# The adaLN rows at the start of a decoder trunk: full-width condition columns, x loaded ahead of w_ada, and another order for the first group

## The chip, the cores and the metric

The kernel runs on one core of a Trainium2 chip. The metric is device time in microseconds from the start to the end of one execution; lower is better.

## What is computed

One layer of a decoder trunk with adaLN conditioning, on 1024 tokens of width 1024, in float32. The change lies at its beginning:

```python
cond = jax.nn.silu(c)                                   # (1, 1024)
mod = cond @ w_ada[layer] + b_ada[layer]                # (1, 6 * 1024)
shift1, scale1, gate1, shift2, scale2, gate2 = jnp.split(mod[:, None, :], 6, axis=-1)
h = rms_norm(x, w_norm1[layer]) * (1.0 + scale1) + shift1
x = x + gate1 * hybrid_mixer(h, w_in[layer], ...)       # h @ w_in, four mixers, @ w_out
h = rms_norm(x, w_norm2[layer]) * (1.0 + scale2) + shift2
x = x + gate2 * hierarchical_moe(h, ...)                # 4 groups of 8 experts, top 2
return rms_norm(x, w_norm_final)
```

Only shift1 and scale1 are needed for the first h, and only they are made in the stage that is changed: 2048 of the 6144 columns of w_ada, 8.4 MB.

## The kernel before

The first stage makes h in transposed form, channels on partitions, as two float32r parts: hH, its rounded value, and hL, the rest. In the same stage the values and gates (272 columns of w_in) are multiplied for all 8 token tiles. Its instructions stand in the order in which the code is written (`tc.manual_schedule()`). Work of later stages that needs nothing of it (the first pieces of w_in, loaded at L134 and split by `split`, L53 and L61) is placed among it by the scheduler.

**x.** `x_load` (L194) brings a tile of 128 tokens; there are 7 buffers, and the two pieces of w_in for the values use the same ones. `x_rows` takes the squares (ScalarE), the root, and scales the rows (VectorE, L246). `x_columns` transposes the tile on TensorE (L253, eight transposes) and copies half of it on ScalarE, half on VectorE (L258) into hT.

**The rows of w_ada.** The 1024 channels go in four groups of 256 (`GS`), group g with 256 columns of shift and 256 of scale. `ada_load(g, q)` brings half of a group's rows of w_ada (L201, two DMAs; three buffers). The product of cond with a group's 512 columns is shared between two engines: for the first `KD = 6` blocks of 128 rows VectorE sums weight times cond into `acc` (`ada_sums`, L210 and L212), and for the last two TensorE multiplies with cond as a stationary operand of one column (`ada_products`). `ada_row` adds the sums over the partitions with a product of `acc` and a column of ones, and ScalarE copies the resulting row out of PSUM (`arow`). `ada_columns` turns the row into columns with four transposes (L232), and VectorE makes shift and scale of them (`sc`, L233 and L235).

**A group's use.** Two ScalarE instructions make hH from hT with scale and shift, two more make the unrounded value, and VectorE subtracts (hL). TensorE then multiplies: `tok_hi`, two products of 128 x 272 for each of 7 token tiles and each of the group's two channel blocks (28 in all), in the middle of which the next group's `ada_products` stand; then that group's `ada_row`; then `tok_lo`, 14 products with hL of the group before. The products with hL are called the low part here, those with hH the wide products, and a float32 product is two records in the trace.

All loads of the stage are issued by SyncE (SP) in one order, which is that of the code.

Of the kernel before, what the change touches and what calls it, by code (L numbers as in the profile page):

```python
# [9 lines left out]
F32 = mybir.dt.float32  # L10
# [9 lines left out]
P = 128  # L20
S = 1024
D = 1024
NT = S // P
KT = D // P
# [12 lines left out]
def hybrid_block_kernel(ctx, tc, x, c, w_in, w_out, w_mix_norm, attn_f_bias, sg_w, sg_b,  # L37
# [4 lines left out]
    nc = tc.nc  # L42
# [9 lines left out]
    def act(o, i, f, **kw):  # L52
        return nc.scalar.activation(o, i, f, **kw)  # L53

    def mm(o, l, r, start, stop):
        return nc.tensor.matmul(o, l, r, start=start, stop=stop)  # L56

    def split(hi, lo, src, eng=None):

        act(hi, src, AF.Copy)  # L60
        (eng or nc.vector).tensor_sub(lo, src, hi.bitcast(F32))  # L61
# [10 lines left out]
    ones = consts.tile([P, P], F32, name="ones")  # L72
# [24 lines left out]
    cond = consts.tile([P, KT], F32, name="cond")  # L97
# [4 lines left out]
    def ps1():  # L102
        return ps.tile([P, 512], F32, name="ps1")

    def pq1():
        return pq.tile([P, 512], F32, name="pq1")
# [45 lines left out]
    def tok_hi(o, w, t, k):  # L152
        wh, wl, n = w
        ts = slice(t * P, (t + 1) * P)
        mm(o[:, :n], hH[:, k, ts], wh[:, k, :n], k == 0, False)
        mm(o[:, :n], hH[:, k, ts], wl[:, k, :n], False, False)

    def tok_lo(o, w, t, k):
        mm(o[:, :w[2]], hL[k // 4][:, k % 4, t * P:(t + 1) * P], w[0][:, k, :w[2]], False, k == KT - 1)
# [21 lines left out]
    with tc.tile_pool(name="st", bufs=1, side="left") as st, tc.tile_pool(name="stx", bufs=7, side="left") as stx, \  # L181
# [7 lines left out]
        xts, was, accs, ada, wraw = {}, {}, {}, {}, {}  # L189
        KD = 6  # L190

        def x_load(t):
            xts[t] = stx.tile([P, D], F32, name="xt", tag="xt")
            nc.sync.dma_start(xts[t], x[t * P:(t + 1) * P])  # L194

        def ada_load(g, q):

            k0, k1 = GS[g]
            was[g, q] = stw.tile([P, 4, 2, (k1 - k0) * P], F32, name=f"wt{k1 - k0}", tag="wt")
            for i in range(2):  # L200
                nc.sync.dma_start(was[g, q][:, :, i], w_ada[q * 4 * P:(q + 1) * 4 * P, i * D + k0 * P:i * D + k1 * P]  # L201
                                  .rearrange("(k p) f -> p k f", p=P))

        def ada_sums(g, k):

            if k == 0:
                accs[g] = st.tile([P, 2, (GS[g][1] - GS[g][0]) * P], F32, name="acc", bufs=2)
            acc, wt = accs[g], was[g, k // 4][:, k % 4]
            if k == 0:
                nc.vector.tensor_scalar(acc, wt, cond[:, k:k + 1], None, op0=OP.mult)  # L210
            else:
                nc.vector.scalar_tensor_tensor(acc, wt, cond[:, k:k + 1], acc, op0=OP.mult, op1=OP.add)  # L212

        def ada_products(g):

            ada[g] = pq1()
            for k in range(KD, KT):
                mm(ada[g][0:1], cond[:, k:k + 1], was[g, k // 4][:, k % 4].rearrange("p i f -> p (i f)"), k == KD, False)

        def ada_row(g):  # L220

            mm(ada[g][0:1], ones[:, 0:1], accs[g].rearrange("p i f -> p (i f)"), False, True)
            ada[g, "row"] = st.tile([1, 512], F32, name="arow", bufs=1)
            act(ada[g, "row"], ada[g][0:1], AF.Copy)

        def ada_columns(g):

            k0, k1 = GS[g]
            ks, n = slice(k0, k1), 2 * (k1 - k0)
            o, row = ada[g], ada[g, "row"]  # L230
            for i in range(n):
                nc.tensor.transpose(o[:, i:i + 1], row[:, i * P:(i + 1) * P], ident[0:1, 0:1])  # L232
            nc.vector.tensor_add(sc[:, :, ks], o[:, :n].rearrange("p (i k) -> p i k", i=2),  # L233
                                 cols[:, 54:70].rearrange("p (i k) -> p i k", i=2)[:, :, ks])
            nc.vector.scalar_tensor_tensor(sc[:, 1, ks], sc[:, 1, ks], 1.0, cols[:, 8 + k0:8 + k1],  # L235
                                           op0=OP.add, op1=OP.mult)

        def values_split(i):
            split(wva[0][:, i * 4:i * 4 + 4], wva[1][:, i * 4:i * 4 + 4], wraw[i])

        def x_rows(t):
            sq = st.tile([P, D], B06, name="sq", bufs=1)
            act(sq, xts[t], AF.Square, accum_out=ss[:, t:t + 1])
            act(rstd[:, t:t + 1], ss[:, t:t + 1], AF.Sqrt, scale=1.0 / D, bias=EPS)
            nc.vector.reciprocal(rstd[:, t:t + 1], rstd[:, t:t + 1])
            nc.vector.tensor_scalar(xts[t], xts[t], rstd[:, t:t + 1], None, op0=OP.mult)  # L246

        def x_columns(t):
            xt = xts.pop(t)
            for hf in range(2):  # L250
                tp = pq1()
                for j in range(4):
                    nc.tensor.transpose(tp[:, j * P:(j + 1) * P],  # L253
                                        xt[:, (hf * 4 + j) * P:(hf * 4 + j + 1) * P], ident)
                dst = hT[hf][:, :, t * P:(t + 1) * P]
                src = tp.rearrange("p (a b) -> p a b", b=P)
                if hf:
                    nc.vector.tensor_copy(dst, src)  # L258
                else:
                    act(dst, src, AF.Copy)  # L260

        def values_load(i):
            wraw[i] = stx.tile([P, 4, 272], F32, name="wraw1", tag="xt")
            o = 0
            for c0, n in ((AV, 260), (MDT, 4), (LI, 8)):
                nc.sync.dma_start(wraw[i][:, :, o:o + n], w_in[i * 512:(i + 1) * 512, c0:c0 + n]
                                  .rearrange("(k p) g -> p k g", p=P))
                o += n

        for t in range(5):  # L270
            x_load(t)
        ada_load(0, 0)
        for t in range(5, 7):
            x_load(t)
        ada_load(0, 1)
        x_load(7)
        values_load(0)
        ada_load(1, 0)
        ada_load(1, 1)
# [14 lines left out]
        nc.vector.tensor_scalar(cond, cond, 1.0, None, op0=OP.add)  # L294
        nc.vector.reciprocal(cond, cond)
        nc.vector.tensor_mul(cond, cond, psc[:, 0:KT])
        for t in range(NT + 1):
            if t < NT:
                x_rows(t)
            if t:  # L300
                x_columns(t - 1)
            if t == 3:
                psc = pq1()
                nc.tensor.transpose(psc[:, :66], rows, ident[:66, :66])
                nc.vector.tensor_copy(cols[:, 8:74], psc[:, :66])
            if t == 7:
                ada_products(0)
            for k in {5: (0, 1), 6: (2,), 7: (3, 4), 8: (5,)}.get(t, ()):
                ada_sums(0, k)
        ada_row(0)  # L310
        values_split(0)
        os = [ps1() for _ in range(PSB)] + [pq1() for _ in range(7 - PSB)]
        NGK = len(GS)
        for g, (k0, k1) in enumerate(GS):
            ks, n = slice(k0, k1), k1 - k0
            if g + 2 < NGK:
                ada_load(g + 2, 0)
                ada_load(g + 2, 1)
            ada_columns(g)
            if g + 1 < NGK:  # L320
                for k in range(KD):
                    ada_sums(g + 1, k)
            if k0 == 4:
                hL.append(hpool.tile([P, KT // 2, S], F32R, name="hL1", tag="hL1"))
            ts, ls = [[z[k // 4][:, k % 4] for k in range(k0, k1)] for z in (hT, hL)]
            for k, a in zip(range(k0, k1), ts):
                act(hH[:, k, :], a, AF.Identity, scale=sc[:, 1, k:k + 1], bias=sc[:, 0, k:k + 1])
            for k, a, l in zip(range(k0, k1), ts, ls):
                act(a, a, AF.Identity, scale=sc[:, 1, k:k + 1], bias=sc[:, 0, k:k + 1])
                nc.vector.tensor_sub(l, a, hH[:, k, :].bitcast(F32))  # L330
            if g == 1:
                values_split(1)

            for k in range(k0, k1):
                for t in range(NT - 1):
                    tok_hi(os[t], wva, t, k)
                if k == k0 and g + 1 < NGK:
                    ada_products(g + 1)
            if g + 1 < NGK:
                ada_row(g + 1)  # L340

            for k in range(*GS[g - 1]) if g else ():
                for t in range(NT - 1):
                    tok_lo(os[t], wva, t, k)
# [828 lines left out]
    with ExitStack() as m4:  # L1173
# [263 lines left out]
        with tc.manual_schedule():  # L1437
# [15 lines left out]
            for t in range(NT):  # L1453
# [6 lines left out]
                if last:  # L1460
                    x1T, f = turned(t - 1)
# [12 lines left out]
                if not last:  # L1474
# [3 lines left out]
                    f = [half(i) for i in range(2)]  # L1478
# [46 lines left out]
                if last:  # L1525
# [6 lines left out]
                    f = half(1)  # L1532
# [12 lines left out]
            t = NT - 1  # L1545
# [10 lines left out]
            a, g, p = r6[0], r6[1], r6[3]  # L1556
# [697 lines left out]
```

## Time and profile before

| | |
|---|---|
| three runs | 1276.84, 1277.37 and 1282.47 us, median 1277.37 |
| the profiled execution | 1279.83 us |
| its span, first to last instruction | 1277.7 us |
| PE busy | 1167.9 us, 91% of the span |
| VectorE (DVE), ScalarE (ACT), GpSimd (POOL) busy | 787.1, 591.2, 302.1 us |
| DMA | 305.48 MB, mean 239 GB/s |
| granted TensorE clock, mean | 0.962 |

The profile is of one execution. All times of rows are microseconds from the start of the span. PE is TensorE's products and PEld its weight loads, which run beside them; products are pipelined and their ends are modelled, so that two neighbours can overlap. A row of the timeline stands for one or several instructions of a kind: start, duration, engine, source line, operation, output and inputs, their shapes, the count, and in brackets the idle time of the engine ahead of it with what ended it. The granted clock is a share of 2.4 GHz.

### The profile page before, as it was taken

What the parts mean: (1) busy time and instruction counts of PE and PEld (TensorE: products, weight loads), DVE (VectorE), ACT (ScalarE), POOL (GpSimd) and SP (SyncE); (2) the same over time, 40 slices, a digit from 0 to 9 for tenths busy, and PEclk for the clock granted to TensorE, in tenths of its full rate; (3) what the DMA queues carried; (4) which work ended last, traced back from release to release, by engine and by line L of the source; (5) the groups of instructions that cost most, each with busy time, mean ns of one, the idle gap of its engine ahead of it and who ended that gap; (6) DMA issues with size and microseconds to landing.
All of it is one profiled execution on the core that took longest, in us unless ns stands there. A gap on an engine that the chain in (4) does not pass through costs nothing. (4 is left out here: it accounts for less than half of the span.)

```text
span 1277.7 us, 18620 instructions
## 1 busy us (share of the span) xinstructions
PE 1167.9 (91%) x6479; PEld 867.1 (68%) x6479; DVE 787.1 (62%) x1457; ACT 591.2 (46%) x913; POOL 302.1 (24%) x305
## 2 busy tenths in 40 slices
PE   5699889999999899999959999899999999999991
PEld 3477677889998788887747744366676657665660
DVE  5656766857743488488878941335654564555674
ACT  5542124354743588344437741224553443554563
POOL 1000000002102277333321942102322132222111
PEclk8899999999999999999969999999999999999996
DMA  9604883232221113575477999999999998999974
GB/s 278 202 17 140 263 276 112 80 86 51 70 64 34 43 62 112 204 267 197 170 295 286 332 325 343 383 390 381 380 386 387 350 385 322 342 368 376 341 267 199
DMA packets 96452, 305.48 MB, mean 239 GB/s; under 512 B 15106, under 2 KB 53756, under 8 KB 71772
## 3 DMA queue, kind: packets, MB, share of 16 engines
q1 hardware_dynamic: 84642, 284.43, 60.4%
q0 software_dynamic: 8464, 17.13, 5.7%
q10 hardware_dynamic: 3242, 2.60, 0.6%
q8 instruction: 57, 0.93, 0.3%
q14 instruction: 47, 0.39, 0.1%
HBM read 283.86 MB, written 32.06 MB: 247 GB/s over the span
## 5 line engine op out<-in xcount | busy, mean ns | idle before, releaser
L56 PE MATMUL ps<-wu,xTs 128*64 128x512 f32 x256 | 121.0, 605 | 1.9 <-DMA wu<-in_w_expert_up_dram 1.9
L56 PE MATMUL ps<-wg,xTs 128*64 128x512 f32 x256 | 120.3, 602 | 2.1 <-DMA wg<-in_w_expert_gate_dram 2.1
L1685 POOL DMA_INDIRECT x_d<-yt,tabi x34 | 62.6, 1841 | 238.7 <-DVE yt L1659 187.6
L56 PE MATMUL ps<-wh,hH 128*128 128x256 f32 (+1 forms) x336 | 97.1, 290 | 12.9 <-ACT hH L53 9.9
L56 PE MATMUL ps<-wl,hH 128*128 128x256 f32 (+1 forms) x336 | 95.6, 285 | 0.0
L56 PE MATMUL ps<-wh,hL 128*128 128x256 f32 (+1 forms) x336 | 93.8, 283 | 0.0
L56 PE MATMUL ps<-hH,wh 128*128 128x512 f32 x224 | 89.0, 397 | 0.4 <-ACT xbc L53 0.4
L56 PE MATMUL ps<-hH,wl 128*128 128x512 f32 x224 | 89.1, 398 | 0.0
L56 PE MATMUL ps<-hL,wh 128*128 128x512 f32 x224 | 88.8, 396 | 0.0
L56 PEld LDWEIGHTS ps<-wh,hH 128*128 128x128 f32 x336 | 64.1, 191 | 20.0 <-ACT hH L53 10.2
L56 PEld LDWEIGHTS ps<-wg,xTs 128*64 128x64 f32 x256 | 32.1, 136 | 58.4 <-issue 52.0
L56 PE MATMUL ps<-split,xTH 128*128 128x512 f32 x200 | 69.4, 403 | 1.1 <-PEq L1905 0.3
L53 ACT ACT_TABLE_LOAD x47 | 60.3, 1283 | 18.4 <-DVE xbc L716 5.9
L53 ACT ACTIVATE xTH<-pq 128x512 fp32r<-128x512 f32 x33 | 18.4, 593 | 105.6 <-PE pq L1700 92.7
L1676 POOL TENSOR_TENSOR yt<-yt,g2bc 128x1024 f32<-128x1024 f32 x14 | 33.7, 2410 | 138.1 <-ACT yt L53 122.0
L56 PEld LDWEIGHTS ps<-wl,hH 128*128 128x128 f32 x336 | 64.0, 190 | 1.8 <-issue 1.7
L56 PE MATMUL ps<-wh,xTH 128*128 128x512 f32 (+1 forms) x156 | 64.1, 411 | 1.1 <-PEq L1905 0.2
L56 PEld LDWEIGHTS ps<-wh,hL 128*128 128x128 f32 x336 | 63.1, 190 | 1.7 <-issue 1.7
L61 DVE TENSOR_TENSOR wl<-wu,wh 128x1024 fp32r<-128x1024 f32 x39 | 47.2, 1223 | 27.2 <-ACT wh L53 26.2
L56 PE MATMUL ps<-wl,xTH 128*128 128x512 f32 (+1 forms) x156 | 61.4, 394 | 0.5 <-DVE wl L61 0.5
L56 PE MATMUL pq<-wd,aTs 128*64 128x512 f32 x256 | 58.8, 596 | 2.8 <-PEq L1893 2.1
L56 PE MATMUL ps<-wh,xTL 128*128 128x512 f32 (+1 forms) x156 | 61.1, 391 | 0.2 <-DVE xTL L61 0.2
(552 smaller groups left out, 3178.7 us busy)
## 6 DMA issues: line engine op xcount, KB each, us to landing
wg<-in_w_expert_gate_dram SPq DMA_DIRECT2D x64, 1024.0 KB
wu<-in_w_expert_up_dram SPq DMA_DIRECT2D x64, 1024.0 KB
wd<-in_w_expert_down_dram SPq DMA_DIRECT2D x64, 1024.0 KB
mw<-in_w_ada_dram SPq DMA_DIRECT2D x32, 512.0 KB
wraw<-in_w_in_dram SPq DMA_DIRECT2D x20, 512.0 KB
xt<-in_x_dram SPq DMA_DIRECT2D x16, 512.0 KB
wt<-in_w_ada_dram SPq DMA_DIRECT2D x16, 512.0 KB
woraw<-in_w_out_dram SPq DMA_DIRECT2D x16, 256.0 KB
```

The lines of the kernel that those rows point to most:

```text
L53: return nc.scalar.activation(o, i, f, **kw)
L56: return nc.tensor.matmul(o, l, r, start=start, stop=stop)
L61: (eng or nc.vector).tensor_sub(lo, src, hi.bitcast(F32))
L1676: nc.gpsimd.tensor_mul(yt[:, on_dve * 512:], yt[:, on_dve * 512:], g2bc[:, on_dve * 512:])
L1685: nc.gpsimd.indirect_dma_start(out=x1_d, out_offset=bass.IndirectOffsetOnAxis(ap=tok, axis=0), in_=yt, in_offset=None, bounds_check=S - 1, ...
```

## The change

Four things are edited. cond is copied to a tile of 128 equal columns for the two blocks that TensorE multiplies, and the sums are multiplied with all 128 columns of ones, so that these products have 128 stationary columns and write 128 equal rows, of which the first is used. All eight x tiles are loaded ahead of the first group's w_ada. Row 0's products stand behind the last tile's transposes, and its sums move to the last two steps of the loop. `ada_columns` follows `ada_row` at once: for group 0 ahead of the split of the values' weights, for the later groups ahead of the low part.

```diff
             for k in range(KD, KT):
-                mm(ada[g][0:1], cond[:, k:k + 1], was[g, k // 4][:, k % 4].rearrange("p i f -> p (i f)"), k == KD, False)
+                mm(ada[g], condb[:, k - KD], was[g, k // 4][:, k % 4].rearrange("p i f -> p (i f)"), k == KD, False)
...
-            mm(ada[g][0:1], ones[:, 0:1], accs[g].rearrange("p i f -> p (i f)"), False, True)
+            mm(ada[g], ones, accs[g].rearrange("p i f -> p (i f)"), False, True)
...
-        for t in range(5):
+        for t in range(NT):
             x_load(t)
         ada_load(0, 0)
-        for t in range(5, 7):
-            x_load(t)
         ada_load(0, 1)
-        x_load(7)
         values_load(0)
...
+        condb = st.tile([P, KT - KD, P], F32, name="condb")
+        nc.vector.tensor_copy(condb, cond[:, KD:, None].to_broadcast([P, KT - KD, P]))
...
-            if t == 7:
-                ada_products(0)
-            for k in {5: (0, 1), 6: (2,), 7: (3, 4), 8: (5,)}.get(t, ()):
+            for k in {7: (0, 1), 8: range(2, KD)}.get(t, ()):
                 ada_sums(0, k)
+        ada_products(0)
         ada_row(0)
+        ada_columns(0)
         values_split(0)
...
-            ada_columns(g)
...
             if g + 1 < NGK:
                 ada_row(g + 1)
+                ada_columns(g + 1)
 
             for k in range(*GS[g - 1]) if g else ():
                 for t in range(NT - 1):
                     tok_lo(os[t], wva, t, k)
```

On SyncE's queue, from the kernel's first load: `xt` is an x tile, `wt` a half of a group's rows of w_ada (two DMAs), `wraw` a piece of w_in, the one of line 134 for the stage behind.

```order
-L194 DMA xt<-in_x_dram 128x1024 x5
-L201 DMA wt_163<-in_w_ada_dram 128x4x256 x2
-L194 DMA xt<-in_x_dram 128x1024 x2
-L201 DMA wt_170<-in_w_ada_dram 128x4x256 x2
+L2249 UNCONDITIONAL_BRANCH
+L194 DMA xt<-in_x_dram 128x1024 x7
+L134 DMA wraw<-in_w_in_dram 128x4x256
 L194 DMA xt<-in_x_dram 128x1024
+L201 DMA wt_169<-in_w_ada_dram 128x4x256 x2
+L201 DMA wt_172<-in_w_ada_dram 128x4x256 x2
 L266 DMA wraw_175<-in_w_in_dram 128x4x260
```

The two w_ada pairs moved behind all eight x tiles, and the scheduler put the first piece of w_in for the next stage ahead of the eighth.

On VectorE, from the copy of the seventh tile's transposes to the sums of group 1: `acc` holds the sums, `sc` shift and scale, `wl` the low part of a weight split.

```order
-L258 COPY hT_149<-pq_348 128x4x128
-L212 SCALAR_TENSOR_TENSOR acc<-wt_170,cond,acc 128x512
+L258 COPY hT_149<-pq_329 128x4x128
+L210 TENSOR_SCALAR acc<-wt_169,cond 128x512
+L212 SCALAR_TENSOR_TENSOR acc<-wt_169,cond,acc 128x512
+L258 COPY hT_149<-pq_344 128x4x128
+L212 SCALAR_TENSOR_TENSOR acc<-wt_169,cond,acc 128x512 x2
+L212 SCALAR_TENSOR_TENSOR acc<-wt_172,cond,acc 128x512 x2
+L233 TENSOR_TENSOR sc<-pq_354,cols 128x2x2
+L235 SCALAR_TENSOR_TENSOR sc<-sc,cols 128x2
 L61 TENSOR_TENSOR wl<-wraw_175,wh 128x1088
-L233 TENSOR_TENSOR sc<-pq_337,cols 128x2x2
-L61 TENSOR_TENSOR wl<-wraw,wh 128x4x256
-L235 SCALAR_TENSOR_TENSOR sc<-sc,cols 128x2
```

Shift and scale moved ahead of both splits, and one of the two splits moved away, behind the group's low-part subtractions.

On TensorE, at the end of group 1's products: `pq_467` is group 2's row, `hL_117` the low part. Before:

```order
L56 MATMUL pq_363<-wh,hL_117 128x272
L56 MATMUL pq_364<-wh,hL_117 128x272
L56 MATMUL pq_365<-wh,hL_117 128x272
L56 MATMUL pq_366<-wh,hL_117 128x272
L232 MATMUL pq_467<-ident,arow 128x1 x4
L56 MATMUL ps_360<-wh,hH 128x272
```

The transposes of the row were the last thing ahead of group 2's wide products. In the change the row is `pq_469`:

```order
L56 MATMUL pq_469<-acc,ones 128x512
L232 MATMUL pq_469<-ident,arow 128x1 x4
L56 MATMUL ps_368<-wh,hL_117 128x272
L56 MATMUL ps_369<-wh,hL_117 128x272
L56 MATMUL pq_370<-wh,hL_117 128x272
```

The transposes now stand right behind the product with the sums, ahead of the 14 low-part products; group 3 reads the same.

## Rows read from the trace of the kernel before

**Rows 1.** The page's 40 slices: busy tenths of TensorE and of DMA.

```profile
PE   5699889999999899999959999899999999999991
...
DMA  9604883232221113575477999999999998999974
```

**Rows 2.** Waits on TensorE, 0 to 90 us: total us, times, longest.

```profile
PE ps L56 <- ACT hH L53: 9.9, 4, 4.5
```

**Rows 3.** Timeline of TensorE from row 0's products on.

```profile
26.83 3.57 PE L56 MATMUL pq<-wt,cond 128*1 128x512 f32 x4
30.34 1.17 PE L253 MATMUL pq<-ident,xt 128*128 128x128 f32 x8
32.95 1.02 PE L56 MATMUL pq<-acc,ones 128*1 128x512 f32 x2 [1.44 <-DVE acc L212]
34.65 0.40 PE L232 MATMUL pq<-ident,arow 1*128 1x1 f32 x4 [0.68 <-ACT arow L53]
39.58 0.59 PE L56 MATMUL ps<-wh,hH 128*128 128x272 f32 x1 [4.53 <-ACT hH L53]
```

**Rows 4.** Timeline of ScalarE, same stretch, and group 1's hH.

```profile
25.41 1.06 ACT L53 ACTIVATE sq<-xt 128x1024 bf16<-128x1024 f32 x1 [1.37 <-DMA xt<-in_x_dram]
...
34.50 2.04 ACT L53 ACTIVATE wh<-wraw 128x1088 fp32r<-128x1088 f32 x2
38.29 2.37 ACT L53 ACTIVATE hH<-hT,sc 128x1024 fp32r<-128x1024 f32 x2 [1.75 <-DVE sc L235]
...
49.96 2.38 ACT L53 ACTIVATE hH<-hT,sc 128x1024 fp32r<-128x1024 f32 x2 [0.95 <-DVE sc L235]
```

**Rows 5.** Timeline of VectorE, same stretch.

```profile
27.03 0.75 DVE L246 TENSOR_SCALAR xt<-xt,rstd 128x1024 f32<-128x1024 f32 x1
...
32.15 0.74 DVE L212 SCALAR_TENSOR_TENSOR acc<-wt,cond,acc 128x512 f32<-128x512 f32 x1
35.62 1.29 DVE L61 TENSOR_TENSOR wl<-wraw,wh 128x1088 fp32r<-128x1088 f32 x1 [2.73 <-ACT wh L53]
...
38.04 0.15 DVE L235 SCALAR_TENSOR_TENSOR sc<-sc,cols 128x2 f32<-128x2 f32 x1
```

**Rows 6.** Windows: stretch, busy us by engine; last three: clock, DMA share, GB/s.

```profile
0.00:13.80 13.80, 4.94 (x23) 4.45 (x24) 7.31 (x32) 8.96 (x19) 5.39 (x17) 1.00 0.80 191
0.00:23.60 23.60, 8.81 (x48) 7.74 (x49) 12.57 (x42) 14.62 (x31) 5.39 (x17) 0.93 0.91 270
0.00:25.20 25.20, 9.71 (x51) 8.27 (x52) 14.13 (x45) 15.06 (x31) 5.39 (x17) 0.90 0.93 272
37.70:44.00 6.30, 4.42 (x16) 3.43 (x17) 6.12 (x10) 5.58 (x5) 0.00 (x0) 0.50 0.74 233
51.10:54.20 3.10, 2.94 (x13) 2.95 (x14) 2.96 (x6) 3.10 (x4) 0.00 (x0) 0.50 0.21 63
64.60:67.80 3.20, 3.20 (x11) 1.47 (x10) 3.13 (x5) 2.21 (x2) 0.00 (x0) 0.51 0.00 0
```

**Rows 7.** Timeline of TensorE, groups 0 to 2.

```profile
47.37 1.02 PE L56 MATMUL pq<-acc,ones 128*1 128x512 f32 x2
...
51.26 0.60 PE L56 MATMUL ps<-wh,hH 128*128 128x272 f32 x1 [1.79 <-ACT hH L53]
...
54.62 1.88 PE L56 MATMUL pq<-wt,cond 128*1 128x512 f32 x4
...
58.38 1.02 PE L56 MATMUL pq<-acc,ones 128*1 128x512 f32 x2
...
63.46 0.40 PE L56 MATMUL ps<-wh,hH 128*128 128x272 f32 x1 [1.79 <-ACT hH L53]
```

**Rows 8.** The tile wt: its weight loads; duration ns least, median, most.

```profile
L56 PEld LDWEIGHTS pq<-wt,cond x16: 79/83/126, 26.8 to 67.6; 128*1 128x1 f32 x16
```

**Rows 9.** The page's costliest groups: busy us, mean ns of one, idle before.

```profile
L56 PEld LDWEIGHTS ps<-wh,hH 128*128 128x128 f32 x336 | 64.1, 191 | 20.0 <-ACT hH L53 10.2
```

**Rows 10.** Waits of SyncE's queue, 0 to 60 us.

```profile
SPq L194 <- PE pq L253: 0.7, 1, 0.7
```

## The prediction

> **What bounds the kernel now.** I read the page's 40 slices first. They show two regimes: from about 700 us on the DMA engines are full in nearly every slice, and before that TensorE is. A slice is 32 us; the first two are the only ones ahead of 600 us with PE under 8 (5 and 6, then 9) [rows 1]. The change edits only that place, so I then read who waits for whom on TensorE in the first 90 us: its costliest wait behind the start is for the scaled rows hH, 9.9 us in 4 waits, the longest 4.5 [rows 2]. There are four column groups, so that is one wait each.
>
> The timeline then shows what the longest consists of. On TensorE the two products of the first w_ada slice start at 26.83 and hold it for 3.57 us; the last x tile's eight transposes stand behind them (30.34); the product with the sums follows at 32.95, four one-column transposes at 34.65, and the first wide product only at 39.58 after 4.53 us idle [rows 3]. On ScalarE the last x tile landed at 25.41, two weight splits run from 34.50 to 36.54, and hH starts at 38.29 [rows 4]. On VectorE the last sum ends at 32.89, because it stands behind the copy of those late transposes, and ahead of the second shift/scale instruction (38.04) come two weight splits, the first of 1.29 us from 35.62 [rows 5]. So row 0 is late by order on three engines, not by arithmetic. Behind the stage no load is short: DMA is at 0 in the third slice and 4 in the fourth, while PE is at 9 [rows 1]. What the stage gains is handed on.
>
> **The loads.** An x tile is 0.52 MB, a w_ada slice pair 1.05 MB. In the old order the last x tile stands behind 7 other x tiles and two pairs, 6.3 MB. DMA moved 270 GB/s x 23.6 us = 6.37 MB by 23.60 [rows 6], and ScalarE could start on the tile at 25.41 [rows 4], so a tile is usable some 1.8 us after its bytes are through. In the new order SyncE also sends one 0.52 MB piece of w_in ahead of the last x tile; the second w_ada pair is usable after 6.3 + 0.5 + small ones = 6.86 MB, which is 272 x 25.2 [rows 6], so at 25.2 + 1.8 = **27.0**. The last x tile has 1.6 MB less ahead of it and comes some 4 us earlier, about 21.3; from there to the end of its scaling it took 2.4 us (25.41 to 27.78) [rows 4, 5], and eight transposes take 1.2 us, twice that at half clock [rows 3]: they are done by 26.1, so w_ada and not x releases the products.
>
> **Row 0's product.** Products from 27.0 for 3.5 us, the time they take now [rows 3], end 30.5. The sums 4 and 5 need 2 x 0.74 us [rows 5] and are done by 29. The product with the sums, 1.02 us, ends at 31.5. Now it ends at 33.97. Gain 2.5 us. Bounds: a gain of 3.9 if the products ran at full clock, where the same four records took 1.88 us [rows 7] and the sums (29.0) come last; a loss of 3.2 if the loads are as late as in the first rival.
>
> **Shift/scale ahead of the splits.** From the end of that product to hH it takes 38.29 - 33.97 = 4.3 us now. In group 1, where nothing stands between, it is 49.96 - 48.39 = 1.6 us [rows 4, 7]. One split (half of 2.04) stays on ScalarE ahead of hH, and 0.6 + 1.0 us of it fits that time, so 1.7. Gain 2.6; I see no bound below 2 or above 2.7. hH then starts at 33.2 and the first wide product 1.3 us later, as now, at 34.5 instead of 39.58. The other split moves behind the group's low-part subtractions, where VectorE waits for TensorE anyway: 0. Its cover is the 7.1 us that TensorE takes for a group's products (51.26 to 58.38) [rows 7]; without it, 1.3.
>
> **The clock.** In group 0 TensorE had idled 4.53 us and then worked at a granted clock of 0.50 (1.2 GHz) from 37.7 to 44.0, 6.3 us [rows 3, 6]. Its pause is now about 3 us with the small transposes in it, which is just group 1's pause (48.39 to 51.26), behind which 3.1 us ran at half [rows 6, 7]. Half of the 3.2 us saved is 1.6. Bounds 0 and 3.1. Group 1 keeps its pause: 0, bounds plus and minus 1.6.
>
> **Transposes ahead of the low part's products** (groups 2 and 3). Now: product with sums ends at 59.40, low part 1.9, transposes 0.4, 1.79 us idle, first wide product at 63.46: 4.06 us [rows 7]. New: wait for the row copy 0.68, transposes 0.40 [rows 3], low part 1.9, in which shift/scale and hH (1.8) are hidden: 3.0. Gain 1.0 each, 2.0 in two groups; bounds 1.5 and 2.2. Group 2 also ran 3.2 us at half clock from 64.6 on, after that idle time [rows 6]; with no pause over 0.7 us I take it as gone: 1.6, bounds 0 and 1.6.
>
> **What it adds.** The copy of cond to 128 columns is one VectorE instruction in its first 8 us, when it has little to do: 0. The 24 weight loads of the w_ada products and sums grow from 1 to 128 columns: 83 ns now, 191 ns for a load of 128 columns, so 24 x 108 ns = 2.6 us if none is hidden [rows 8, 9]. But 14 wide products took 1.88 us (56.50 to 58.38), 134 ns each, less than one of their loads lasts [rows 7, 9]: loads run beside products. I take 0.3, bounds 0 and 2.6. The Trainium skill (TensorE: Matmul & The Clock Gate, "LDWEIGHTS (loading the stationary operand)") speaks against this edit: a load's time grows with the columns, columns over 1.2 in ns, an estimated 107 ns each for 128. By that rule alone, loads in line, the sum below would be 7.7 us; the spacing of the trace's products decides against it.
>
> **Sum.** 2.5 + 2.6 + 1.6 + 2.0 + 1.6 - 0.3 = **10.0 us**. The profiled execution took 1279.83 us (span 1277.7), which gives 1269.8; the median of the three runs, 1277.37, is 2.5 us below it, so I say **1267.4**. It should carry to the end: TensorE is the bound from 75 us to 600, and the expert loads that fill DMA behind it are released by what it finished.
>
> **Rivals.** (1) *w_ada becomes row 0's wait.* For: all of it now stands behind 4.7 MB, and the first 13.8 us moved only 191 GB/s [rows 6]. If the x tiles and the w_in piece went at that rate throughout, 4.75 MB would take 24.9 us where the forecast's rate needs 19.2, 5.7 us later; gain 4.3, time 1273. Against: from 14 us on it speeds up, as 270 GB/s over 23.6 us implies. Chance 0.18. (2) *Swallowed later.* The DMA-full last half absorbs the shift, because a transfer and not TensorE sets its start. For: its slices are full. Against: they fill only after 670 us. Gain 0 to 3, time about 1276. Chance 0.14. (3) *The clock stays up everywhere*, since the products and sums now run back to back ahead of a short pause: 1.4 (row 0's products), 1.5 (group 0) and 1.6 (group 1) on top, gain 14.5, time 1262.9. Against: the same pause let it fall in group 1. Chance 0.12. (4) *Slower: SyncE stands at the last x load with all of w_ada behind it.* There are 7 x buffers, so this load waits for tile 0's transposes. That wait was 0.7 us [rows 10], and 1.5 MB is queued on DMA behind which it hides. It decides only once DMA has run dry: each us more is a us of w_ada, and beyond 10 us it is slower; at 17 us, 1284. Chance 0.06, with it that the change does less than its order says.
>
> **How the numbers follow.** The forecast has what is left, 0.50, its own range is 1265 to 1270. The range that should hold 8 in 10 takes in rival 3 and most of rival 1: 1262 to 1274.5. A measurement here tells 0.5%, 6.4 us, from no change. Faster by more: 0.50 + 0.12 and a fifth of rival 1, 0.66. Slower by more: 0.06. The same: 0.28.
>
> **What would show it.** In the new profile: the first wide product near 34.5, w_ada's products starting near 27 with no transposes behind them; both shift/scale instructions ahead of the split on VectorE; 3.0 us from product with sums to the next wide product in groups 2 and 3; half clock in group 0 for some 3 us and none in group 2; the first product of the next projection about 10 us earlier. It is wrong if the products start after 30, if half clock stays 6 us, or if that first product is earlier by 10 us and the end is not.

## The result and the profile after

The changed kernel takes 1268.19 us, median of 6 runs (1265.99 to 1269.53), against 1277.37: a ratio of 0.9919, interval 0.9900 to 0.9938. In a second comparison it is 0.9929 (0.9908 to 0.9951). The forecast was 1267.4.

The stage is best measured by where the next one begins, its first product of 128 x 512. It began at 86.02 us and now begins at 75.37, 10.65 us earlier. On TensorE's timeline of the kernel before:

```profile
86.02 0.40 PE L56 MATMUL ps<-hH,wh 128*128 128x512 f32 x1
```

The changed kernel:

```profile
25.99 3.65 PE L56 MATMUL pq<-wt,condb 128*128 128x512 f32 x4 [2.38 <-DMA wt<-in_w_ada_dram]
29.46 1.04 PE L56 MATMUL pq<-acc,ones 128*128 128x512 f32 x2
...
33.44 0.59 PE L56 MATMUL ps<-wh,hH 128*128 128x272 f32 x1 [1.85 <-ACT hH L53]
...
40.06 1.02 PE L56 MATMUL pq<-acc,ones 128*128 128x512 f32 x2
...
43.96 0.60 PE L56 MATMUL ps<-wh,hH 128*128 128x272 f32 x1 [1.79 <-ACT hH L53]
...
47.30 3.21 PE L56 MATMUL pq<-wt,condb 128*128 128x512 f32 x4
...
52.08 1.02 PE L56 MATMUL pq<-acc,ones 128*128 128x512 f32 x2
53.78 0.41 PE L232 MATMUL pq<-ident,arow 1*128 1x1 f32 x4 [0.68 <-ACT arow L53]
...
55.98 0.40 PE L56 MATMUL ps<-wh,hH 128*128 128x272 f32 x1
...
61.33 1.02 PE L56 MATMUL pq<-acc,ones 128*128 128x512 f32 x2
...
75.37 0.40 PE L56 MATMUL ps<-hH,wh 128*128 128x512 f32 x1
```

These answer to [rows 3, 7]. Row 0's products wait for w_ada, as the brackets of the first line say, and no transposes stand behind them. The first wide product starts at 33.44 after 1.85 us idle instead of 39.58 after 4.53. Groups 2 and 3 start without any pause in brackets. Group 1 is the odd one: from its first wide product (43.96) to the product with the sums (52.08) it takes 8.12 us, where it took 7.12. The windows, which answer to [rows 6], show why; the last three columns are granted clock, DMA share and GB/s:

```profile
33.00:36.30 3.30, 2.86 (x12) 2.86 (x13) 3.16 (x6) 3.30 (x4) 0.00 (x0) 0.50 1.15 296
43.30:49.90 6.60, 5.94 (x18) 4.40 (x19) 6.46 (x8) 5.95 (x6) 0.00 (x0) 0.50 0.90 293
54.00:75.00 21.00, 20.32 (x147) 18.37 (x147) 10.85 (x28) 12.55 (x16) 0.57 (x2) 1.00 0.04 12
```

Group 0 now has half clock (1.2 GHz) for 3.3 us instead of 6.3, but group 1 has it for 6.6 instead of 3.1, and from 54 us on there is none. In sum the two groups have as much of it as before (9.9 us against 9.4); what is gone is group 2's.

On VectorE, shift and scale now stand ahead of the only split left there (compare [rows 5]), and hH on ScalarE follows at 32.14:

```profile
31.69 0.16 DVE L233 TENSOR_TENSOR sc<-pq,cols 128x4 f32<-128x4 f32 x1 [3.55 <-PE pq L232]
31.89 0.16 DVE L235 SCALAR_TENSOR_TENSOR sc<-sc,cols 128x2 f32<-128x2 f32 x1
32.16 1.29 DVE L61 TENSOR_TENSOR wl<-wraw,wh 128x1088 fp32r<-128x1088 f32 x1
```

The timeline of ScalarE in the changed kernel:

```profile
32.14 2.38 ACT L53 ACTIVATE hH<-hT,sc 128x1024 fp32r<-128x1024 f32 x2
```

The lead is handed on. The load of a router bias, some 420 us later on the timeline of SyncE's queue, in the kernel before:

```profile
505.60 0.33 SPq L1188 DMA_DIRECT2D rbias<-in_b_router_group_dram  x1
```

The changed kernel:

```profile
495.60 0.33 SPq L1187 DMA_DIRECT2D rbias<-in_b_router_group_dram  x1
```

10.0 us are left there, and 9.2 in the medians at the end (12.4 between the spans of the two profiled executions, 1277.7 and 1265.3 us).

### The profile page after: what moved, and what is told of

Same layout as the page of the kernel before. It is cut to its first block, busy times and chain, and to the rows that moved or that the text cites. A ratio compares the mean times of both kernels' runs of the same rounds, so it can differ in the third digit from the quotient of the medians.

```text
span 1265.3 us, 18621 instructions
## 1 busy us (share of the span) xinstructions
PE 1161.8 (92%) x6479; PEld 869.3 (69%) x6479; DVE 788.1 (62%) x1458; ACT 591.8 (47%) x913; POOL 301.9 (24%) x305
## 5 line engine op out<-in xcount | busy, mean ns | idle before, releaser
L61 DVE TENSOR_TENSOR wl<-wu,wh 128x1024 fp32r<-128x1024 f32 x39 | 47.2, 1222 | 27.2 <-ACT wh L53 26.1
L53 ACT ACTIVATE sg<-ps 128x512 f32<-128x512 f32 (+1 forms) x32 | 19.0, 593 | 89.9 <-PE ps L56 48.6
```

## The experiments

Each kernel was profiled. The measure is the start of the next stage's first product; the time with its ratio to the kernel before stands beside it. Medians of kernels that differ by 1 or 2 us don't tell them apart, the stage does.

**The changed kernel again.**

> The changed kernel once more, nothing edited, to see how far its first stage repeats. Theory (the stage's order sets its length, only the stretches at half clock move): the first product of the next projection starts at 75.4 us as in its first profile, within 1.6 us either way, and the time is 1268 us. Rival (the 10.65 us of the first profile are partly luck of the clock): that product starts anywhere from 75 to 80 us.

76.74 us; 1269.25 us. Within the theory's 1.6 us either way, and within the rival's range too. Row 0's products started at 27.41 instead of 25.99, because w_ada landed later, and this time group 0 had the long stretch at half clock (34.56 to its sums at 42.66, 8.1 us) and group 1 the short one (6.9), as windows:

```profile
33.80:40.30 6.50, 5.74 (x17) 4.33 (x18) 6.32 (x9) 5.05 (x5) 0.00 (x0) 0.50 1.11 322
47.40:50.60 3.20, 3.20 (x12) 2.59 (x11) 3.13 (x4) 3.20 (x4) 0.00 (x0) 0.50 0.45 131
```

That is the kernel before's division, 6.3 and 3.1 us: the change moved the half clock of these two groups about and did not shorten it. Over the eight profiles with these loads the products started from 25.45 to 27.73; that and the clock make differences of about 1 us in the stage mean nothing, unless they are read within one group.

**One column again.**

```diff
-mm(ada[g], condb[:, k - KD], ...)        mm(ada[g], ones, ...)
+mm(ada[g][0:1], cond[:, k:k + 1], ...)   mm(ada[g][0:1], ones[:, 0:1], ...)
```

> The changed kernel with one stationary column in the w_ada products and sums again; all else as changed. Theory from the new trace (a product of one column and a weight load of 128 columns don't overlap, so each return to the wide products waits for the end of the last record and then for a load, about 0.5 us, and entering costs 0.1): three groups at 0.5 to 0.6 us and the sums on top, the first product of the next projection at 77.0 to 77.6 us instead of 75.4, the time 1269.5. Rival of the prediction (128 columns cost what their loads take, 0.3 us): 75.1 us, the time 1268. Rival on the clock (only full-width products keep the clock up): more than one stretch at half clock longer by over 3 us and that product after 78.5 us.

77.12 us; 1268.01 us, ratio 0.9922 (0.9892 to 0.9951). Within the theory's range in the stage, while the time can't tell. The clean measure is group 2, which ran at full clock in both: 5.73 us from its first wide product (57.36) to its sums (63.09), against 5.35. So 128 columns are 0.4 us a group faster, not slower. The weight loads on the timeline show how. In group 1 of the kernel before:

```profile
55.48 0.08 PEld L56 LDWEIGHTS pq<-wt,cond 128*1 128x1 f32 x1 [0.35 <-issue]
56.43 0.19 PEld L56 LDWEIGHTS ps<-wh,hH 128*128 128x128 f32 x1 [0.86 <-ACT wh L53]
```

The changed kernel:

```profile
37.44 0.19 PEld L56 LDWEIGHTS pq<-wt,condb 128*128 128x128 f32 x1 [0.24 <-issue]
37.86 0.19 PEld L56 LDWEIGHTS ps<-wh,hH 128*128 128x128 f32 x1 [0.24 <-ACT wh L53]
```

Behind the last product of one column the first load of 128 columns comes after 0.95 us, behind that of 128 columns after 0.42. The ScalarE instruction that the bracket of the 0.86 us names had ended at 55.60, so it is not what the load waited for.

**64 columns.** The changed kernel with `ada[g][0:64]`, `condb[:, k - KD, 0:64]` and `ones[:, 0:64]`.

> The changed kernel with 64 stationary columns in the w_ada products and sums. Theory (the next load of 128 columns overlaps the last product only where both have the same columns): as with one column, about 0.4 us per group at full clock more than with 128: group 2 takes 5.7 us from its first wide product to its product with the sums instead of 5.35. Rival (any wide enough stationary overlaps): 5.35 us.

77.34 us; 1268.48 us in one run. Group 2, at full clock, takes 5.78 us (57.48 to 63.26), as with one column. The load of 128 columns again waits:

```profile
60.34 0.14 PEld L56 LDWEIGHTS pq<-wt,condb 128*64 128x64 f32 x1 [0.29 <-issue]
61.29 0.19 PEld L56 LDWEIGHTS ps<-wh,hH 128*128 128x128 f32 x1 [0.81 <-ACT hT L53]
```

So 64 columns are no better than one here. But it is no rule that both sides must have 128 columns. Further on in the kernel before stand products of 72 columns whose operands are float32r and which are one record each, and a load of 128 columns starts beside them:

```profile
540.71 0.23 PE L56 MATMUL pq<-x1TH,wrs 128*72 128x128 f32 x1
540.72 0.19 PEld L56 LDWEIGHTS ps<-wo11H,yH 128*128 128x128 f32 x1
```

Which of the two, the columns or the kind of product, makes this difference is open.

**The columns alone**, in the kernel before, profiled twice, and **the kernel before again**.

> The kernel before with 128 stationary columns in the w_ada products and sums and nothing else. Theory (a return from one column to 128 exposes a load and the last record's end): 0.4 to 0.5 us per group, the first product of the next projection at 83.8 to 84.8 us instead of 86.0, give or take 1.6 us for the clock; the time 1275.5 to 1277. Rival of the prediction (more columns, longer loads): 86.3 to 88.6 us, the time 1278 to 1280.

81.63 us; 1273.89 us, ratio 0.9984 (0.9966 to 1.0002), which doesn't exclude no change. In the stage it is more than either side expected, 4.4 us. Group 2 gives 2.0 of them: it took 5.34 us instead of 7.33, 0.4 less by the overlap and 1.6 because it ran at full clock behind the same pause of 1.79 us. Groups 0 and 1 give 0.9 and 0.5, the earlier end of row 0's product 0.6 (33.36 against 33.97), and the low part, which follows the product with the sums sooner, 0.2 twice.

> The kernel before, unedited, profiled once more: does group 2 start at half clock again (64.6 to 67.8 us in its first profile), behind a pause of 1.8 us and with products of one stationary column ahead? Theory (pause and one column together let the clock fall): yes, 3 us or more of half clock between 61 and 69 us, and the first product of the next projection at 85.5 to 86.5 us. Rival (chance of when the chip looks): no half clock there, that product 1.6 us earlier.

> The kernel before with 128 columns alone, profiled once more: does group 2, behind the same pause of 1.8 us, stay at full clock as in its first profile? Theory (products of 128 columns ahead of the pause hold the clock up through it): no half clock behind 58 us, and the first product of the next projection at 81 to 83 us. Rival (chance): half clock there, that product at 83.5 us or later.

86.69 and 81.83 us; one run each, 1278.12 and 1276.31 us. Group 2, from its first wide product to its product with the sums, in all six profiles in which it has that pause, as windows. With one column, first the kernel before:

```profile
63.50:70.80 7.30, 7.30 (x33) 4.40 (x34) 5.92 (x14) 3.31 (x3) 0.66 (x2) 0.77 0.01 2
```

The kernel before again:

```profile
64.10:71.50 7.40, 7.35 (x33) 4.44 (x34) 6.01 (x14) 3.40 (x4) 0.66 (x2) 0.77 0.00 0
```

The loads alone:

```profile
63.80:71.10 7.30, 7.30 (x32) 4.48 (x32) 5.96 (x14) 3.35 (x3) 0.66 (x2) 0.77 0.00 0
```

With 128 columns, first the columns alone:

```profile
61.20:66.60 5.40, 5.36 (x33) 4.40 (x34) 5.29 (x9) 3.39 (x3) 0.56 (x2) 1.00 0.00 0
```

The columns alone, again:

```profile
61.50:66.80 5.30, 5.30 (x33) 4.34 (x34) 5.19 (x8) 3.30 (x3) 0.57 (x2) 1.00 0.00 0
```

The low part first:

```profile
57.50:62.90 5.40, 5.35 (x32) 4.39 (x33) 5.29 (x9) 3.40 (x3) 0.57 (x2) 1.00 0.00 0
```

Three of three fell with one column and none of three with 128. It isn't shown that the columns hold the clock up through this pause. Group 1's pause is as long, and there the clock fell with 128 columns too, each time. Group 3's is 1.79 us as well, and there it stayed at full with one column too, in all three profiles; the kernel before, where group 3's wide products start at 75.88:

```profile
73.90:86.00 12.10, 10.31 (x84) 10.22 (x83) 3.88 (x11) 7.67 (x12) 0.00 (x0) 1.00 0.00 0
```

And in the three profiles with one column group 2's clock fell at the same place, 1.1 to 1.2 us behind its first wide product, so they are hardly three separate draws.

**The loads alone**, in the kernel before.

> The kernel before with all of x loaded ahead of w_ada and nothing else. Theory (row 0's products still stand ahead of the last tile's transposes, and now wait for w_ada, so the x that came early waits with them): products from about 27 us, transposes behind them at 30.5, the sums' product at 33 to 34.5, the first product of the next projection at 85.5 to 87.5 us; the time 1277 to 1279. Rival (early x is worth its 5 us by itself): 81 to 84 us, the time 1273 to 1275.

86.35 us; 1278.56 us, ratio 1.0007 (0.9992 to 1.0021). The theory's numbers came out: early x alone is worth nothing. But what it waits behind is not the products. VectorE's first sum waits for w_ada, with the scaling of the seventh and eighth tiles behind it, and TensorE waits for that scaling:

```profile
23.28 0.49 DVE L210 TENSOR_SCALAR acc<-wt,cond 128x512 f32<-128x512 f32 x1 [3.78 <-DMA wt<-in_w_ada_dram]
25.56 1.94 PE L253 MATMUL pq<-ident,xt 128*128 128x128 f32 x8 [5.45 <-DVE xt L246]
```

Row 0's products follow at 27.44 with no wait for w_ada. The product with the sums starts at 33.44 instead of 32.95. In the changed kernel the sums stand behind the scaling of the last tile.

**The old loads** in the changed kernel.

> The changed kernel with the loads in their old order: x tiles 0 to 4, half of the first w_ada, tiles 5 and 6, the other half, tile 7. Theory (with row 0's products and four sums behind the last tile, that tile's landing now sets row 0): tile 7 lands at 25.4 us instead of 19.9 or earlier, its copies end near 30.5, four sums of 0.75 us behind them, the product with the sums ends near 34.8 instead of 30.5, and the first product of the next projection starts at 79.0 to 80.0 us; the time is 1272. Rival (w_ada's landing sets row 0 in either order and the gain comes from the order of the instructions alone): 75.4 to 76.4 us and 1268 to 1269.

77.54 us; 1270.83 us, ratio 0.9939 (0.9920 to 0.9958). Neither. The last x tile was usable at 23.78, not at 25.4 as in the kernel before, though the loads stand in the same order there: SyncE issued it 1.6 us earlier (13.50 against 15.11), and why is open. Its transposes were out of the way at 27.2, and the sums behind their copy ended at 31.5; the product with the sums started at 31.61 after a wait for the sums, against 29.46 and 30.60. x does set row 0 with the old loads, but the price is 1 to 2 us, not 4.

**The split first** (`values_split(0)` ahead of `ada_columns(0)`).

> The changed kernel with the values' split ahead of group 0's transposes and shift/scale, as before; the scheduler then puts the second split back there too. Theory (2.6 us of the gain were the splits in row 0's way): from the end of row 0's product with the sums to hH 4.3 us instead of 1.6, the first product of the next projection at 78 to 80 us, the time 1271. Rival (the wide products wait for the values' split anyway, so its place doesn't matter): hH later but the first wide product no later than 34.6 us, that product at 75.4 to 76.8, the time 1268 to 1269.

76.57 us; 1270.17 us, ratio 0.9944 (0.9927 to 0.9961). The stage misses the theory's range, and both of the rival's signs came out (a first wide product at 34.22, the stage within its range), but only since w_ada came early here and the products with it ran at full clock: the product with the sums ended at 28.61, 1.9 us ahead of the changed kernel's. From there to hH it took 4.31 us (32.92) instead of 1.64, so the step itself is worth 2.7, and to the first wide product 5.6 instead of 2.9, of them 4.54 idle. By these lengths the rival, that the product waits for the split anyway, falls.

**The low part first** (`ada_columns(g)` at the head of the loop for g of 1 to 3).

> The changed kernel with the row's transposes of groups 1 to 3 back at the head of the next group, behind the low part; group 0's stay ahead of the split. Theory (the low part hides the shift/scale and hH): groups 2 and 3 lose 1.2 us each, and a pause of 1.8 us comes back ahead of their wide products, with which group 2 or 3 may start at half clock again, 1.6 us more; the first product of the next projection at 78.5 to 81 us (75.4 and 76.7 in the two profiles of the changed kernel), the time 1272. Rival (the order only swaps two things that TensorE has to do anyway): 75.4 to 77 us, the time 1268 to 1269.

77.95 us; 1270.88 us, ratio 0.9945 (0.9923 to 0.9968). The stage lies between the two ranges. From the end of the product with the sums to the next first wide product group 2 takes 3.88 us and group 3 3.88, against 2.88: 1.0 each, so 2.0. No half clock came back with the pause, in which the theory's upper end lay.

**Each group's own low part.** A version that the new trace suggests: the low part of a group stands behind its own wide products, so that group 1's row has cover too.

```diff
-            for k in range(*GS[g - 1]) if g else ():
+            for k in range(k0, k1) if g + 1 < NGK else ():
                 for t in range(NT - 1):
                     tok_lo(os[t], wva, t, k)
```

> The changed kernel with each group's low part multiplied behind its own wide products instead of behind the next group's, so that group 1's row also has 14 products beside it. Theory (group 1's pause of 1.8 us ahead of its wide products is pure waiting, and the half clock of 6.6 us follows from it): 1.8 us less pause and about 3 us less half clock, the first product of the next projection at 70 to 72.5 us instead of 75.4, the time 1264. Rival (the low part waits for its subtractions on VectorE, which end at 40.1 us in group 0 and later in group 1, so the wait only moves): 75 to 77 us, the time 1268 to 1270.

71.51 us; **1262.84 us**, ratio 0.9883 (0.9845 to 0.9921), 6.4 us below the changed kernel in the same comparison. Its timeline:

```profile
40.75 1.02 PE L56 MATMUL pq<-acc,ones 128*128 128x512 f32 x2
42.45 0.41 PE L232 MATMUL pq<-ident,arow 1*128 1x1 f32 x4 [0.68 <-ACT arow L53]
42.78 0.52 PE L56 MATMUL ps<-wh,hL 128*128 128x272 f32 x2
...
44.66 0.39 PE L56 MATMUL ps<-wh,hH 128*128 128x272 f32 x1
...
49.97 1.02 PE L56 MATMUL pq<-acc,ones 128*128 128x512 f32 x2
```

Group 1 now starts without a pause and takes 5.3 us at full clock instead of 8.1. VectorE had the subtractions done at 40.37, ahead of the transposes, so the rival's wait isn't there.

**Group 0's pause filled**, in that version: two products of `ones` and the sums into PSUM tiles that the wide products then start afresh. Their results are used by nothing.

> The kernel with each group's own low part, and in group 0's pause (from the row's transposes to the first wide product, 1.85 us) two products of 128 x 512 whose results nothing reads. Theory (a pause on TensorE brings the stretch at half clock that group 0 ran from 35.0 to 38.5 us): at full clock the two take 1.7 us and fit the pause, no half clock behind 33 us, the first product of the next projection at 69.5 to 70.5 us instead of 71.5. Rival (the clock falls there for another reason, or the extra products themselves run at half clock): that product at 71.5 to 73.5 us.

70.66 us; 1263.24 us, ratio 0.9906 (0.9875 to 0.9938). Group 0's windows, first in each group's own low part, without them:

```profile
33.70:40.70 7.00, 6.94 (x32) 5.15 (x33) 6.82 (x10) 4.35 (x5) 0.00 (x0) 0.76 1.12 329
```

With them:

```profile
34.40:39.80 5.40, 5.40 (x34) 4.40 (x34) 5.22 (x8) 4.34 (x4) 0.00 (x0) 1.00 1.11 301
```

The pause was the cause of the half clock: without it group 0 takes 5.4 us and not 7.0. It is one profile, but in all thirteen others, where TensorE pauses ahead of group 0 for 1.85 us or 4.5, group 0 ran in part at half clock, and here none follows up to the next stage (a granted clock of 1.00 from 31 to 71 us). From the end of row 0's product with the sums to the next stage it is 39.2 us instead of 40.7. The total falls short of the theory's 70.5 only because row 0's product ended 0.7 us later, and the median can't tell the two versions apart.

## Why the prediction was right

The time (0.8 us off), the sign and the stage's gain (10.0 said, 10.65 and 9.3 in the two profiles) came out as forecast. The waits and the order were right; that the sum is so close is in part luck, as one term that did not come was made up by one that the sum had with the wrong sign. Point by point, in the first and in the second profile of the changed kernel:

| step | said | first | second | from |
|---|---|---|---|---|
| the loads and row 0's product | 2.5 | 3.5 | 2.4 | its end 30.50 and 31.62 against 33.97 |
| shift/scale ahead of the splits | 2.6 | 2.7 | 2.7 | 1.64 against 4.32 us to hH |
| clock in group 0 | 1.6 | 1.2 | -0.3 | 6.62 and 8.10 against 7.79 us, overlap included |
| clock in group 1 | 0 | -1.0 | 0.2 | 8.12 and 6.91 against 7.12 us, overlap included |
| transposes ahead of the low part | 2.0 | 2.4 | 2.4 | 2.88 against 4.06 and 4.07 us |
| clock in group 2 | 1.6 | 2.0 | 2.0 | 5.35 and 5.33 against 7.33 us, overlap included |
| longer weight loads | -0.3 | +0.4 per group | +0.4 per group | inside the lines above; one_column, columns_64 |

- *The loads* were right in mechanism: w_ada and not x releases the products (bracket at 25.99). The forecast's 27.0 lies within what eight profiles gave, 25.45 to 27.73; the first profile's 25.99 was early by luck. Rival 1, w_ada 5.7 us later, didn't occur in any. The experiments add what the sum didn't say: the loads are worth nothing alone, since the sums then hold up the scaling of the last two tiles, and 1 to 2 us with the sums and the products behind the last tile.
- *The split* and *the low part* were right in size, and undoing each cost that: 2.7 and 2.0 us.
- *"I take 0.3, bounds 0 and 2.6"* for the longer weight loads failed in sign. The bound "0" left out a gain, though the row was there to see: between the last one-column load and the next wide one the weight loads idled 0.86 us. The loads are hidden: the four records of a row's products take 1.88 us at full clock with either kind. The hand-over that they replace was not hidden. The loads themselves did grow, the tile's median from 83 to 200 ns. That a load's time grows with the columns is the rule of the Trainium skill (TensorE: Matmul & The Clock Gate, "LDWEIGHTS (loading the stationary operand)"); by its formula a load of 128 columns takes an estimated 107 ns, where this trace has 187 at least.
- *The clock in group 0* is the step that failed. The prediction had it that a pause as short as group 1's would bring a half clock as short as group 1's. In the first profile it did, but group 1's grew by as much; in the second group 0 had 6.5 us of it, which the prediction named as a sign of being wrong. The two groups together took 14.9 us and now take 14.7 and 15.0, though the overlap alone is worth 0.8: nothing of the 1.6 us is there. What stands in for it in the sum is the overlap, 1.2 us in three groups, and the 0.3 us that the loads did not cost. Even a half clock of 3.1 us would not have brought 1.6: of the 6.3 us 1.9 had been idle time (37.7 to 39.58), in which a lower clock costs nothing, and half of the working time saved in the first profile is 0.8.
- *"With no pause over 0.7 us I take it as gone"* for group 2: gone it is, but the reason isn't the only one. With 128 columns it stayed up behind the full pause three times of three, and with 1 or 64 columns it stayed up without the pause (5.73 and 5.78 us). The two edits cover the same 1.6 us, which is why the undoings cost less than what the columns give alone.
- *Group 1's* minus 1.0 lies within its bounds of plus and minus 1.6.
- Rival 2, swallowed later, falls: 10.0 us are there at 500 us and 9.2 at the end. Rival 4 falls: the last x load was issued at 10.74, behind a wait of 2.0 us, with DMA full. Rival 3, the clock up everywhere, falls too: it takes other edits to bring part of it. own_low_part brings it in group 1 and filled_pause in group 0 as well, but even there row 0's products ran at half clock (3.55 us).

## What to carry to other kernels

When a small product feeds a wide stage, look at what stands behind it in program order on every engine: here the transposes, two splits and the low part each made row 0 or its successors wait, and moving the short chain ahead of the long work that doesn't need it gave what was worked out from the waits. Moving loads alone moves nothing while the instructions that need them stand behind others. And cover every pause, the odd group too: the pause that was left cost its own length and again as much in clock.

## What the runs showed of the hardware

- A weight load of 128 columns did not run beside a float32 product (two records) of 1 or of 64 columns, but did beside one of 128: 0.95 against 0.42 us from load to load, 0.4 us per group of products. It did start beside float32r products (one record) of 72 columns.
- Behind a pause of 1.8 us group 2 ran at half clock for some 3 us in 3 of 3 profiles with one column, and in 0 of 3 with 128. Why group 1's like pause ended at half clock in either case, and group 3's in neither, stays open.
- Two products without use, put into a pause of 1.85 us, kept the clock at full and won 1.5 us of the stage, in one profile.
